# Ten pairs of k-tiles with seven products instead of eight, weight sums made by accumulating DMAs, residual kept in DRAM

## The chip, the cores and the metric

The kernel runs on one core of a Trainium2 chip. The metric is the device time of one launch in microseconds (us). The engines of the core have names in the profile: PE is TensorE (matmuls), PEld its weight loads, DVE is VectorE, ACT is ScalarE, POOL is GpSimd and SP is SyncE, which here only issues DMAs. Each engine works through its own queue in order and waits on semaphores.

## The reference

One layer of a hybrid decoder, for 256 tokens of width 2048, all in float32. A first half mixes tokens by three branches (a gated convolution, a gated MLP over chunks, a sparse attention), projects with `w_o`, normalises and adds the result to the input. The second half is the feed-forward network, and the change lies there:

```python
h = rms_norm(x, norm_ffn_pre[l])
u = causal_depthwise_conv(h @ w_up[l], ffn_conv_w[l], ffn_conv_b[l])
u_g, u_v = jnp.split(u, 2, axis=-1)
x = x + rms_norm((jax.nn.silu(u_g) * u_v) @ w_down[l], norm_ffn_post[l])
```

The product with `w_down` has 256 tokens, an inner dimension of 5632 (44 k-tiles of 128) and 2048 columns. `x` on the right of the last line is the residual: it is known before the feed-forward network begins and is needed again only at its very end.

## The kernel before, in words

Every float32 operand of a matmul is split into a rounded high part (ACT copies it into a type that TensorE runs fast) and a low part (DVE subtracts the high part from the original). A product is three matmuls: high by high, high by low, low by high. Weights arrive as tiles `wraw` of 128 x 1024 (512 KB, five buffers, fetched by SP), and the split parts go into rings `whi` and `wlo` of four buffers each. A fetch waits for the DVE step that last read the buffer five tiles before; a split waits for TensorE to finish with the ring buffer four before.

The up stage computes `h @ w_up` for 88 tiles of 128 features, two per k-tile: the convolution, `silu` and the product follow on ACT and DVE, and the result for each k-tile is stored split, in `gh` and `gl`. `fsum`, `small`, `sums` and the loop over `NFT` (L1177 to L1202) do this.

The down stage multiplies with `w_down`. Tokens are taken in two halves of 128 (`H1`, `H2`), columns in two halves of 1024 (`Pair(0)`, then `Pair(1)`), each as two blocks of 512 (`L`, `U`). A *plain* k-tile is four products (two token halves by two column blocks), 12 matmuls of 512 columns. A *quad* takes two k-tiles together: a 2 x 2 by 2 x 2 block product, which would be eight products, done with seven (the Strassen-Winograd scheme), 21 matmuls. It needs four weight arrays of 128 x 1024 at most: `b` as it lies in memory, `a` and `tt` with sums and differences, and a last half array; and, per pair, three sums and one difference of activations. Eight pairs of the 44 k-tiles are quads (`EARLY`, five pairs, and `LATE`, three), 28 tiles are plain (`PLAIN`).

The activation sums of the `EARLY` pairs are made in the up stage by `sums` and kept in `se`. There was no room for more, so those of the `LATE` pairs are made by `late` in the first column half of the down stage from `gh` and `gl`, into `sl`. The four weight combinations of a quad are made on DVE in `quad` (L1283, L1284, L1287, L1290): `b` is fetched as a `wraw` tile, `a` into `qa` (one buffer), and the combinations go into `qa` and into `tt`, one of two areas of `fin` that `scratch` gives in turn.

The order of DVE and ACT in the down stage is written out by hand (`fixed` chains each instruction behind the one before it on the engine), as is that of TensorE (`in_line`). The lists in the two loops say how many plain tiles come before each quad. The order of SP's and POOL's queues is found by the framework's scheduler. Six plain tiles of the second column half (`KEEP`) are split early and multiplied last. `combine` adds the seven products' sums up, `result` and `weigh` finish each block, and at the end the residual `y1`, which has been in SBUF since before the up stage, is added (L1402) and the output stored.

Of the kernel before, what the change touches and what calls it, by code (L numbers as in the profile page):

```python
# [20 lines left out]
F32 = mybir.dt.float32  # L24
# [10 lines left out]
NFT = FF // 128  # L35
EPS = 1e-6

EARLY = [(0, 1), (2, 3), (4, 5), (6, 7), (8, 9)]
LATE = [(11, 12), (13, 14), (15, 16)]
PLAIN = [*range(22, 33), 10, *range(17, 22), *range(33, NFT)]  # L40
BA, BB, BC, BG = 2100, 2200, 2200, 2500
PR = 1000
NW0, _ = 9, 6
# [12 lines left out]
def block(ctx: ExitStack, tc: tile.TileContext, x, xf, fp, cst, rows, sgw, w1, w2, wf_a, wt_bv, wf_bu, wf_c,  # L56
# [1054 lines left out]

    P2 = ctx.enter_context(tc.tile_pool(name="p2", bufs=1))
    P2b_ctx = ExitStack()
    se = P2.tile([128, 2, len(EARLY), 3, 128], R, name="se")
# [18 lines left out]
    with ExitStack() as order:  # L1133
        order.enter_context(tc.high_priority())
        for ins in seq[V] + seq[S]:
            order.enter_context(tc.issue_after(ins))
        junk3 = small("junk3", (128, 512), mybir.dt.bfloat16)
        for t in range(2):
            for c in range(4):
                xc = y1[:, t, c * 512:c * 512 + 512]  # L1140
                if c % 2:
                    V.scalar_tensor_tensor(junk3, xc, 1.0, xc, op0=ALU.mult, op1=ALU.mult,
                                           accum_out=ss2[:, t, c:c + 1])
                else:
                    S.activation(junk, xc, AF.Square, accum_out=ss2[:, t, c:c + 1])
        r2 = norm1(ss2, "f", 2)
    pu2.append(PS.tile([128, 2, T], F32, tag="acc", name="pu2"))
    for run in lumps(pu2[2], hs, h2):
        in_line(run)
# [15 lines left out]
    def sums(st, a0, a1, k0, dst, do=loose):  # L1165

        h, l = g2(k0, H2)
        do(V, V.tensor_add, st[:, 1], a0[:, H2], a1[:, H2])
        do(V, V.tensor_sub, st[:, 2], st[:, 1], a0[:, H1])
        do(V, V.tensor_sub, st[:, 3], a1[:, H1], st[:, 2])  # L1170
        do(S, S.activation, dst[0], st[:, 1:4], AF.Copy)
        do(V, V.tensor_sub, st[:, 0], a0[:, H1], a0[:, H2])
        do(S, S.activation, h, st[:, 0], AF.Copy)
        do(V, V.tensor_sub, dst[1], st[:, 1:4], dst[0].bitcast(F32))
        do(V, V.tensor_sub, l, st[:, 0], h.bitcast(F32))

    for i in range(NFT):  # L1177
        acc = []
        for v in range(2):
            f = 2 * i + v  # L1180
            with tc.issue_after(pe_last[0]):
                pu = pu2[f] if f < 3 else ftile(wf_up[f], h2)
            s = P2b.tile([128, T], F32, tag="fs", bufs=2, name=f"fs{f}")
            fsum(pu, s, rb=rb2)
            a = small(f"fa{f}")
            w = [fps[:, C_FW + f * 3 + k:C_FW + f * 3 + k + 1] for k in range(3)]
            S.activation(a, s, AF.Identity, bias=fps[:, C_FB + f:C_FB + f + 1], scale=w[2])
            V.scalar_tensor_tensor(a[:, 1:T], s[:, 0:T - 1], w[1], a[:, 1:T], op0=ALU.mult, op1=ALU.add)
# [4 lines left out]
        ts = H1 if i in [k for k, _ in EARLY] else slice(0, T)  # L1193
# [3 lines left out]
        for j, (k0, k1) in enumerate(EARLY):  # L1197
            if i == k0:
                first = acc[0]
            elif i == k1:  # L1200
                st = P2b.tile([128, 4, 128], F32, tag="st", name=f"st{j}")
                sums(st, first, acc[0], k0, (se[:, 0, j], se[:, 1, j]))  # L1202
    P2b_ctx.close()


# [6 lines left out]
    sl = P2c.tile([128, 2, len(LATE), 3, 128], R, name="sl")  # L1212
# [6 lines left out]
    PAIRS = EARLY + LATE  # L1219
# [23 lines left out]
    class Pair:  # L1243
# [24 lines left out]
                    in_line(self.mm, self.c[t][n], g2(PLAIN[i], (H1, H2)[t]), (hi[:, c], lo[:, c]),  # L1268
                            self.p == 0 and i == len(PLAIN) - 1)

        def quad(self, j):

            k0, k1 = PAIRS[j]
            last = j == len(PAIRS) - 1
            L, U = slice(0, 512), slice(512, 1024)
            b = fetch(wt_dq[self.p, j][:, 0:1024], 1024)
            a = P2c.tile([128, 1024], F32, name=f"qa{self.p}_{j}", tag="qa", bufs=1)
            nc.sync.dma_start(a, wt_dq[self.p, j][:, 1024:])
            nm = f"q{self.p}_{j}"
            tt = scratch()  # L1280
            (hb, lb), (ha, la), (ht, lt), (h4, l4) = (ring(nm + x) for x in "bat4")
            high(hb, b)
            fixed(V, V.tensor_sub, tt[:, L], b[:, L], a[:, U])  # L1283
            fixed(V, V.tensor_sub, a[:, U], a[:, U], a[:, L])  # L1284
            high(ha, a)
            rest(lb, b, hb)
            fixed(V, V.tensor_sub, tt[:, U], b[:, L], a[:, U])  # L1287
            high(ht, tt[:, 0:1024])
            rest(la, a, ha)
            fixed(V, V.tensor_sub, tt[:, 1024:], b[:, U], tt[:, U])  # L1290
            high(h4[:, L], tt[:, 1024:])
            rest(lt, tt[:, 0:1024], ht)
            rest(l4[:, L], tt[:, 1024:], h4[:, L])
            src, n = (se, j) if j < len(EARLY) else (sl, j - len(EARLY))
            s1, s2, s4 = ((src[:, 0, n, i], src[:, 1, n, i]) for i in range(3))
# [12 lines left out]
        def combine(self):  # L1308

            fixed(S, S.activation, self.at(0, 0), self.p1, AF.Copy)  # L1310
            fixed(V, V.tensor_add, self.at(1, 0), self.p6, self.at(0, 0))
            fixed(V, V.tensor_add, self.at(0, 1), self.p5, self.at(1, 0))
            fixed(V, V.tensor_add, self.at(1, 1), self.p7, self.at(0, 1))
            fixed(V, V.tensor_add, self.at(1, 0), self.p7, self.at(1, 0))

        def result(self, t, n, do):

# [17 lines left out]
    def late(j):  # L1335
        k0, k1 = LATE[j]
        tmp = scratch()
        a = tmp[:, 0:512].rearrange("p (k t) -> p k t", k=2)
        gi, gk = divmod(k0, 11)
        fixed(V, V.tensor_add, a, gh[gi][:, gk:gk + 2].bitcast(F32), gl[gi][:, gk:gk + 2].bitcast(F32))  # L1340
        sums(tmp[:, 512:1024].rearrange("p (s t) -> p s t", s=4), a[:, 0], a[:, 1], k0, (sl[:, 0, j], sl[:, 1, j]), fixed)

    NP, NQ, KEEP = len(PLAIN), len(PAIRS), 6


    first, second = Pair(0), None
    i = 0
    for j in range(NQ):
        while i < (6, 9, 13, 17, 19, 21, 23, 25)[j]:
            first.plain(i)  # L1350
            i += 1
        if 1 <= j <= len(LATE):
            late(j - 1)
        first.quad(j)
    for i in range(i, NP):
        first.plain(i)
# [2 lines left out]
    kept = []  # L1359
    i = 0  # L1360
    for j in range(NQ):
        while i < 3 + -((3 + KEEP - NP) * j // (NQ - 1)):
            second.plain(i)
            if i == 2:
                for t in range(2):
# [17 lines left out]
    for t in range(2):  # L1383
# [15 lines left out]
        for c in range(4):  # L1399
            for x, w in ((c * 512, 512),) if c < 3 or t == 0 else ((1536, 256), (1792, 256)):  # L1400
                cc = slice(x, x + w)
                V.scalar_tensor_tensor(res[:, t, cc], res[:, t, cc], r3, y1[:, t, cc], op0=ALU.mult, op1=ALU.add)  # L1402
                nc.sync.dma_start(out[t, :, cc], res[:, t, cc])


def _layout(inp):
# [66 lines left out]
    k0, k1 = [k for k, _ in EARLY + LATE], [k for _, k in EARLY + LATE]  # L1473
    quads = np.concatenate([dn[:, k1, 1], dn[:, k1, 0], dn[:, k0, 0], dn[:, k0, 1]], axis=3)


# [40 lines left out]
```

## Time and profile before

| | us |
|---|---|
| median of 3 runs | 1578.95 |
| lowest, highest | 1578.72, 1579.39 |
| the profiled execution, its time | 1579.09 |
| its span in the profile | 1577.3 |
| TensorE busy | 1566.0 |
| DVE busy | 1213.9 |
| ACT busy | 884.9 |
| up stage ends, down stage begins (TensorE) | 1338.2 |
| second column half begins | 1453.6 |
| last matmul of the down stage ends | 1567.9 |

The page and the views of the trace give times from the span's start. The granted TensorE clock is at full speed over the whole span. Busy times of different engines overlap. A matmul is recorded with 0.39 us, but the next one starts 0.23 us later, so the step from start to start tells more than the busy time does. In rows of tiles the three numbers behind a count are the shortest, the median and the longest of one, in ns.

### The profile page before, as it was taken

How to read it: one execution, taken by the hardware profiler on the slowest of the kernel's cores; microseconds unless marked ns; L12 is line 12 of the kernel's file. 1: busy time of each engine (PE TensorE's matmuls, PEld its weight loads, DVE VectorE, ACT ScalarE, POOL GpSimd, SP SyncE). 2: the span in 40 equal slices, each digit the busy share in tenths (PEclk: the TensorE clock that was granted, in tenths of full speed). 3: DMA queues.
4: the chain of work that ended last, by engine and by line, in shares of the span. 5: the costliest groups of instructions: out<-in, count | busy, mean ns of one | idle time of the engine just before them, and what ended most of it. 6: DMA issues, size and time to landing. Idle time of an engine off the chain costs nothing.

```text
span 1577.3 us, 22324 instructions
## 1 busy us (share of the span) xinstructions
PE 1566.0 (99%) x8185; PEld 1330.1 (84%) x8185; DVE 1213.9 (77%) x2081; ACT 884.9 (56%) x1430; POOL 18.2 (1%) x46
## 2 busy tenths in 40 slices
PE   9999999999999999999999999999999999999997
PEld 7888889888888787788888888888888888788886
DVE  8899999857865555465558988777777777888887
ACT  7544454447637675544456665555555555556563
POOL 1000020000000000000000000000000000000000
PEclk9999999999999999999999999999999999999999
DMA  9555566666765545565773666666666666656672
GB/s 376 186 192 181 186 177 213 194 192 184 235 202 152 156 145 162 161 195 183 247 242 105 203 187 189 189 191 189 192 187 191 189 191 192 204 194 214 214 243 77
DMA packets 84862, 303.74 MB, mean 193 GB/s; under 512 B 9744, under 2 KB 10768, under 8 KB 84240
## 3 DMA queue, kind: packets, MB, share of 16 engines
q1 hardware_dynamic: 83376, 297.71, 60.0%
q0 software_dynamic: 944, 4.19, 0.8%
q8 instruction: 64, 1.05, 0.3%
q10 hardware_dynamic: 432, 0.41, 0.1%
q14 instruction: 46, 0.38, 0.1%
HBM read 299.13 MB, written 2.10 MB: 191 GB/s over the span
## 4 chain that ended last, share of the span: by engine, by line
PE 98%; DVE 1%; DMA 1%; ACT 0%; issue 0%; DVEq 0%; SPq 0%; ACTq 0%
PE ps L173 29%; PE ps L180 15%; PE pd1a L1259 6%; PE pg L194 6%; PE pg L193 6%; PE pg L195 6%; PE pd0b L1259 5%; PE py L194 3%; PE py L195 3%; PE py L193 3%; PE po L195 2%; PE po L194 2%; PE po L193 2%; PE pd1b L1259 1%; PE pd0a L1259 1%; PE pv L193 1%
## 5 line engine op out<-in xcount | busy, mean ns | idle before, releaser
L145 DVE TENSOR_TENSOR wlo<-wraw,whi 128x1024 fp32r<-128x1024 f32 x440 | 534.9, 1218 | 171.6 <-ACT whi L144 164.4
L144 ACT ACTIVATE whi<-wraw 128x1024 fp32r<-128x1024 f32 x440 | 461.2, 1053 | 242.1 <-PE pg L195 96.7
L173 PE MATMUL ps<-h2T,whi 128*128 128x512 f32 x1360 | 325.0, 391 | 0.0
L173 PEld LDWEIGHTS ps<-h2T,whi 128*128 128x128 f32 x1360 | 249.8, 188 | 48.2
L180 PEld LDWEIGHTS ps<-h2T,wlo 128*128 128x128 f32 x1360 | 174.5, 191 | 6.7
L180 PE MATMUL ps<-h2T,wlo 128*128 128x256 f32 x1360 | 176.6, 283 | 0.0
L173 PE MATMUL ps<-hT,whi 128*128 128x512 f32 x640 | 157.4, 392 | 0.0
L215 ACT ACTIVATE t<-ps 128x256 f32<-128x256 f32 x125 | 47.6, 382 | 188.1 <-PE ps L173 188.0
L195 PE MATMUL pg<-whi,hT 128*128 128x512 f32 x384 | 150.9, 393 | 0.0
L194 PE MATMUL pg<-wlo,hT 128*128 128x512 f32 x384 | 150.7, 392 | 0.0
L193 PE MATMUL pg<-whi,hT 128*128 128x512 f32 x384 | 147.6, 393 | 0.0
L173 PEld LDWEIGHTS ps<-hT,whi 128*128 128x128 f32 x640 | 116.0, 189 | 21.3
L216 DVE TENSOR_TENSOR t<-ps,t 128x256 f32<-128x256 f32 x125 | 52.5, 421 | 79.0 <-ACT t L215 78.7
L476 DVE SCALAR_TENSOR_TENSOR cv<-hb,fps,cv 128x256 f32<-128x256 f32 x240 | 104.7, 475 | 0.2 <-ACT cv L472 0.2
L180 PEld LDWEIGHTS ps<-hT,wlo 128*128 128x128 f32 x640 | 84.7, 190 | 4.7
L180 PE MATMUL ps<-hT,wlo 128*128 128x256 f32 x640 | 86.8, 283 | 0.0
L194 PEld LDWEIGHTS pg<-wlo,hT 128*128 128x128 f32 x384 | 72.1, 188 | 16.1 <-issue 1.1
L195 PEld LDWEIGHTS pg<-whi,hT 128*128 128x128 f32 x384 | 72.1, 188 | 15.1 <-issue 0.7
L193 PEld LDWEIGHTS pg<-whi,hT 128*128 128x128 f32 x384 | 71.8, 188 | 14.8 <-issue 0.3
L981 DVE TENSOR_TENSOR wlowraw<-wraw,whiwraw 128x1024 fp32r<-128x1024 f32 x52 | 62.6, 1222 | 15.4 <-ACT whiwraw L981 13.8
L981 ACT ACTIVATE whiwraw<-wraw 128x1024 fp32r<-128x1024 f32 x52 | 54.7, 1059 | 22.4 <-PE pd0b L1259 7.2
L1191 ACT ACTIVATE fa<-fa 128x256 f32<-128x256 f32 x44 | 18.3, 415 | 62.5 <-DVE fa L1189 62.5
(891 smaller groups left out, 2455.4 us busy)
## 6 DMA issues: line engine op xcount, KB each, us to landing
wraw<-in_wf_up_dram SPq DMA_DIRECT2D x176, 512.0 KB, 4.3
wraw<-in_wt_g_dram SPq DMA_DIRECT2D x96, 512.0 KB, 4.3
wraw<-in_wt_dn_dram SPq DMA_DIRECT2D x56, 512.0 KB, 4.5
wraw<-in_wt_p_dram SPq DMA_DIRECT2D x48, 512.0 KB, 4.4
wraw<-in_wf_a_dram SPq DMA_DIRECT2D x32, 512.0 KB, 4.3
wraw<-in_wt_o_dram SPq DMA_DIRECT2D x32, 512.0 KB, 4.6
wraw<-in_wf_bu_dram SPq DMA_DIRECT2D x16, 512.0 KB, 4.4
wraw<-in_wf_c_dram SPq DMA_DIRECT2D x16, 512.0 KB, 4.5
```

What stands on the lines that cost most here:

```text
L144: S.activation(hi[:, :n], raw[:, :n], AF.Copy)
L145: V.tensor_sub(lo[:, :n], raw[:, :n], hi[:, :n].bitcast(F32))
L173: ins = PE.matmul(ps[:, :, ts], lhsT=ws[k // 8][0][:, c:c + 128], rhs=mov[:, k, :, ts], start=(k == 0 and not t), stop=(k == n - 1), skip_ ...
L180: ins = PE.matmul(ps[:, 1, ts], lhsT=ws[k // 8][1][:, c:c + 128], rhs=mov[:, k, 0, ts], start=False, stop=False, skip_group_check=True).ins
L193: PE.matmul(ps, lhsT=xh, rhs=hi, start=first, stop=False)
L194: PE.matmul(ps, lhsT=xh, rhs=lo, start=False, stop=False)
L195: return PE.matmul(ps, lhsT=xl, rhs=hi, start=False, stop=last).ins
L215: S.activation(t1, ps[:, 1], AF.Copy)
L216: V.tensor_add(t1 if rb is not None else dst, ps[:, 0], t1)
L476: V.scalar_tensor_tensor(ca[:, j], hb[:, j, k:k + T], w(j, k), ca[:, j], op0=ALU.mult, op1=ALU.add)
L981: seq[eng] = [op(*args, **kw).ins]
L1259: ins = PE.matmul(bank, lhsT=a[x], rhs=w[y], start=first and j == 0, stop=last and j == 2).ins
```

## The change

The pairs become ten, all with their activation sums made in the up stage; 24 k-tiles stay plain. `late` and `sl` go.

- *Room.* `y1` is written to a DRAM tensor `spill` by two DMAs of 1 MB on SP near the start of the up stage. Its place in SBUF takes `sf`, the activation sums of pairs five to nine. After the sixth quad of the second column half, in which these pairs come first, the place is free again, and the residual is read into it (`back`, two DMAs of 1 MB on SP). The second column half takes the pairs in another order for that reason.
- *Weight sums.* `qa` has three buffers. Two of the four combinations are made by DMAs that add: after `a` has been fetched, a DMA from POOL's queue adds 128 x 512 of the weights in DRAM onto its upper half; and the lower half of `tt` is fetched by SP and then added to in the same way. Each is 256 KB. To make all four combinations sums, signs move: the activation sums, two DVE steps of the quad and the last steps of `combine` change between addition and subtraction.
- *Order.* Eight plain tiles come before the first quad instead of six, and the lists that place the quads are new.

```diff
-EARLY = [(0, 1), (2, 3), (4, 5), (6, 7), (8, 9)]
-LATE = [(11, 12), (13, 14), (15, 16)]
-PLAIN = [*range(22, 33), 10, *range(17, 22), *range(33, NFT)]
+PAIRS = [(0, 1), (2, 3), (4, 5), (6, 7), (8, 9), (11, 12), (13, 14), (15, 16), (17, 18), (19, 20)]
+PLAIN = [*range(22, 33), 21, 10, *range(33, NFT)]
...
+    DR = ctx.enter_context(tc.tile_pool(name="dram", bufs=1, space=bass.MemoryType.DRAM))
+    spill = DR.tile([128, 2, D], F32, name="spill")
+    for t in range(2):
+        nc.sync.dma_start(spill[:, t], y1[:, t])
+    sf = P0.tile([128, 2, 5, 3, 128], R, tag="s16", name="sf")
...
-        do(V, V.tensor_add, st[:, 1], a0[:, H2], a1[:, H2])
+        do(V, V.tensor_sub, st[:, 1], a0[:, H2], a1[:, H2])
...
-        do(V, V.tensor_sub, st[:, 3], a1[:, H1], st[:, 2])
+        do(V, V.tensor_add, st[:, 3], a1[:, H1], st[:, 2])
...
-        def quad(self, j):
+        def quad(self, n):
+            j = (n + 5 * self.p) % len(PAIRS)
...
-            a = P2c.tile([128, 1024], F32, name=f"qa{self.p}_{j}", tag="qa", bufs=1)
+            a = P2c.tile([128, 1024], F32, name=f"qa{self.p}_{j}", tag="qa", bufs=3)
             nc.sync.dma_start(a, wt_dq[self.p, j][:, 1024:])
+            G.dma_start(a[:, U], wt_dq[self.p, j][:, 1024:1536], accum_op=ALU.add)
             nm = f"q{self.p}_{j}"
             tt = scratch()
+            nc.sync.dma_start(tt[:, L], wt_dq[self.p, j][:, 1536:])
+            G.dma_start(tt[:, L], wt_dq[self.p, j][:, 0:512], accum_op=ALU.add)
...
-            fixed(V, V.tensor_sub, tt[:, L], b[:, L], a[:, U])
-            fixed(V, V.tensor_sub, a[:, U], a[:, U], a[:, L])
...
-            fixed(V, V.tensor_sub, tt[:, U], b[:, L], a[:, U])
+            fixed(V, V.tensor_add, tt[:, U], b[:, L], a[:, U])
...
-            fixed(V, V.tensor_sub, tt[:, 1024:], b[:, U], tt[:, U])
+            fixed(V, V.tensor_add, tt[:, 1024:], b[:, U], tt[:, U])
...
-        while i < (6, 9, 13, 17, 19, 21, 23, 25)[j]:
+        while i < (8, 9, 11, 13, 14, 16, 17, 19, 20, 21)[j]:
...
-        if 1 <= j <= len(LATE):
-            late(j - 1)
...
-        while i < 3 + -((3 + KEEP - NP) * j // (NQ - 1)):
+        while i < (3, 5, 7, 9, 10, 12, 14, 15, 17, 18)[j]:
...
+        if j == 5:
+            back = s16(P0, [128, 2, D], F32, "back")
+            for t in range(2):
+                nc.sync.dma_start(back[:, t], spill[:, t])
...
-                V.scalar_tensor_tensor(res[:, t, cc], res[:, t, cc], r3, y1[:, t, cc], op0=ALU.mult, op1=ALU.add)
+                V.scalar_tensor_tensor(res[:, t, cc], res[:, t, cc], r3, back[:, t, cc], op0=ALU.mult, op1=ALU.add)
```

More of the change, by code (lines that the diff above doesn't have):

```diff
@@ L1113, in block @@
     P2b_ctx = ExitStack()
-    se = P2.tile([128, 2, len(EARLY), 3, 128], R, name="se")
+    se = P2.tile([128, 2, 5, 3, 128], R, name="se")
     gh = [P2.tile([128, 11, T], R, tag="gh", bufs=4, name=f"gh{i}") for i in range(4)]
@@ L1192, in block @@
         V.tensor_mul(acc[0], acc[0], acc[1])
-        ts = H1 if i in [k for k, _ in EARLY] else slice(0, T)
+        ts = H1 if i in [k for k, _ in PAIRS] else slice(0, T)
         h, l = g2(i, ts)
@@ L1196, in block @@
         V.tensor_sub(l, acc[0][:, ts], h.bitcast(F32))
-        for j, (k0, k1) in enumerate(EARLY):
+        for j, (k0, k1) in enumerate(PAIRS):
             if i == k0:
@@ L1201, in block @@
                 st = P2b.tile([128, 4, 128], F32, tag="st", name=f"st{j}")
-                sums(st, first, acc[0], k0, (se[:, 0, j], se[:, 1, j]))
+                sums(st, first, acc[0], k0, [(se, sf)[j // 5][:, x, j % 5] for x in range(2)])
     P2b_ctx.close()
@@ L1211, in block @@
     gain = fin[:, 4096:5120]
-    sl = P2c.tile([128, 2, len(LATE), 3, 128], R, name="sl")
     turn = [0]
@@ L1217, in scratch @@
         return fin[:, 5120 + 1536 * turn[0]:6656 + 1536 * turn[0]]
-    PAIRS = EARLY + LATE
     ss3 = PZ.tile([128, 2, 8], F32, name="ss3")
@@ L1269, in plain @@
                             self.p == 0 and i == len(PLAIN) - 1)
-        def quad(self, j):
+        def quad(self, n):
+            j = (n + 5 * self.p) % len(PAIRS)
             k0, k1 = PAIRS[j]
-            last = j == len(PAIRS) - 1
+            last = n == len(PAIRS) - 1
             L, U = slice(0, 512), slice(512, 1024)
             b = fetch(wt_dq[self.p, j][:, 0:1024], 1024)
-            a = P2c.tile([128, 1024], F32, name=f"qa{self.p}_{j}", tag="qa", bufs=1)
+            a = P2c.tile([128, 1024], F32, name=f"qa{self.p}_{j}", tag="qa", bufs=3)
             nc.sync.dma_start(a, wt_dq[self.p, j][:, 1024:])
+            G.dma_start(a[:, U], wt_dq[self.p, j][:, 1024:1536], accum_op=ALU.add)
             nm = f"q{self.p}_{j}"
             tt = scratch()
+            nc.sync.dma_start(tt[:, L], wt_dq[self.p, j][:, 1536:])
+            G.dma_start(tt[:, L], wt_dq[self.p, j][:, 0:512], accum_op=ALU.add)
             (hb, lb), (ha, la), (ht, lt), (h4, l4) = (ring(nm + x) for x in "bat4")
             high(hb, b)
-            fixed(V, V.tensor_sub, tt[:, L], b[:, L], a[:, U])
-            fixed(V, V.tensor_sub, a[:, U], a[:, U], a[:, L])
             high(ha, a)
             rest(lb, b, hb)
-            fixed(V, V.tensor_sub, tt[:, U], b[:, L], a[:, U])
+            fixed(V, V.tensor_add, tt[:, U], b[:, L], a[:, U])
             high(ht, tt[:, 0:1024])
             rest(la, a, ha)
-            fixed(V, V.tensor_sub, tt[:, 1024:], b[:, U], tt[:, U])
+            fixed(V, V.tensor_add, tt[:, 1024:], b[:, U], tt[:, U])
             high(h4[:, L], tt[:, 1024:])
@@ L1293, in quad @@
             rest(l4[:, L], tt[:, 1024:], h4[:, L])
-            src, n = (se, j) if j < len(EARLY) else (sl, j - len(EARLY))
-            s1, s2, s4 = ((src[:, 0, n, i], src[:, 1, n, i]) for i in range(3))
+            src = (se, sf)[j // 5]
+            s1, s2, s4 = ((src[:, 0, j % 5, i], src[:, 1, j % 5, i]) for i in range(3))
             for bank_, act, (h, l), c in (
@@ L1311, in combine @@
             fixed(V, V.tensor_add, self.at(1, 0), self.p6, self.at(0, 0))
-            fixed(V, V.tensor_add, self.at(0, 1), self.p5, self.at(1, 0))
-            fixed(V, V.tensor_add, self.at(1, 1), self.p7, self.at(0, 1))
+            fixed(V, V.tensor_sub, self.at(0, 1), self.p5, self.at(1, 0))
             fixed(V, V.tensor_add, self.at(1, 0), self.p7, self.at(1, 0))
+            fixed(V, V.tensor_sub, self.at(1, 1), self.at(0, 1), self.p7)
         def result(self, t, n, do):
@@ L1333, in weigh @@
             do(V, V.tensor_mul, self.at(t, n), self.at(t, n), gain[:, n * 512:n * 512 + 512])
[L1335 to L1341, printed above, removed]
     NP, NQ, KEEP = len(PLAIN), len(PAIRS), 6
@@ L1472, in _layout @@
     plain = c(dn[:, PLAIN].transpose(0, 1, 3, 2, 4)).reshape(2, len(PLAIN), 128, 1024)
-    k0, k1 = [k for k, _ in EARLY + LATE], [k for _, k in EARLY + LATE]
+    k0, k1 = [k for k, _ in PAIRS], [k for _, k in PAIRS]
     quads = np.concatenate([dn[:, k1, 1], dn[:, k1, 0], dn[:, k0, 0], dn[:, k0, 1]], axis=3)
```

## The prediction

> **What bounds the kernel now.** I read the page's busy times first, then the chain of work that ended last, then busy times by stretches, and last the tiles of the stage that the change rewrites.
>
> ```profile
> span 1577.3 us, 22324 instructions
> PE 1566.0 (99%) x8185; PEld 1330.1 (84%) x8185; DVE 1213.9 (77%) x2081; ACT 884.9 (56%) x1430; POOL 18.2 (1%) x46
> PE 98%; DVE 1%; DMA 1%; ACT 0%; issue 0%; DVEq 0%; SPq 0%; ACTq 0%
> ```
>
> TensorE works for 1566.0 of 1577.3 us and makes up 98% of the chain. So a matmul removed is time won, and a transfer, a DVE or an ACT step costs nothing until TensorE waits for it. The chain in the last stage (columns: start, length, what):
>
> ```profile
> 1338.23 5.46 PE pd0b L1259 x24
> ...
> 1346.47 5.64 DMA qa<-in_wt_dq_dram
> ...
> 1352.23 0.70 DVE fin L981
> ...
> 1358.31 1.43 PE pd0a L1259 x5
> ...
> 1453.61 9.52 PE pd1a L1259 x42
> 1463.13 2.72 PE pd1b L1259 x12
> ...
> 1550.85 17.01 PE pd1a L1259 x75
> ...
> 1567.88 0.42 DVE fin L1326
> ```
>
> The stage runs from 1338.23 to 1567.86; column half 1 begins at 1453.61. Twelve matmuls take 2.72 us, so one takes 0.2267. A plain k-tile is 12 matmuls (2.72 us), a quad, which covers two k-tiles with seven products, is 21 (4.76 us).
>
> ```profile
> core 0: us, PE busy (x) PEld busy (x) DVE busy (x) ACT busy (x) POOL busy (x), PEclk, DMA share, GB/s
> 14.00:40.00 26.00, 26.00 (x116) 21.56 (x115) 24.59 (x50) 21.88 (x50) 5.78 (x9) 1.00 1.01 409
> 1338.23:1453.61 115.38, 115.17 (x505) 94.30 (x505) 98.43 (x124) 63.31 (x71) 0.00 (x0) 1.00 0.64 204
> 1453.61:1567.86 114.25, 114.24 (x504) 94.25 (x503) 97.00 (x117) 62.85 (x76) 0.00 (x0) 1.00 0.57 185
> ```
>
> Each half holds 28 plain tiles and 8 quads: 336 + 168 = 504 matmuls, 504 x 0.2267 = 114.25 us. The second half takes exactly that; the first takes 115.38, so 1.13 us are lost in it. Their place shows in TensorE's own rows around the first quad:
>
> ```profile
> 1354.16 0.39 PE L1259 MATMUL pd0b<-whiwraw,gl 128*128 128x512 f32 x1
> 1354.39 0.39 PE L1259 MATMUL pd0b<-whiq_0b,se 128*128 128x512 f32 x1
> 1354.84 0.50 PE L1259 MATMUL pd0b<-wloq_0b,se 128*128 128x512 f32 x1
> ```
>
> The step from 1354.39 to 1354.84 is 0.45, not 0.23: TensorE waits for the first quad's pieces, which are late because the array `qa` landed at 1352.11 (1346.47 + 5.64) and DVE stood until then. The busy sum hardly shows it, as a matmul's 0.39 overlaps the next.
>
> **The change part by part.** *Matmuls.* Ten pairs and 24 plain tiles make 288 + 210 = 498 matmuls a half, 112.89 us, against 504. Twelve matmuls go, on the path: -2.72 us.
>
> *The start of the stage.* Eight plain tiles precede the first quad in place of six. The products of `a` are then due at 1338.23 + 8 x 2.72 + 1.36 = 1361.35. What delivers `a` gets a further hop: SP issues the three `qa` fetches at the same place as before, behind one weight fetch, and POOL then issues a DMA that adds 256 KB onto its upper half. No accumulating transfer is in the trace. Its bounds are POOL's own transfers and the fetches:
>
> ```profile
> L981 DVE TENSOR_TENSOR qa<-qa x16: 691/692/694, 1353.0 to 1542.6; 128x512 f32<-128x512 f32 x16
> L981 DVE TENSOR_TENSOR fin<-wraw,qa x32: 680/684/691, 1352.2 to 1544.3; 128x512 f32<-128x512 f32 x32
> DMA to landing us min/median/max: 3.6/3.8/5.6
> ...
> L937 POOL DMA_DIRECT2D x<-in_x_dram x2: 537/542/548, 755.2 to 755.7; - x2
> DMA to landing us min/median/max: 7.1/8.7/10.2
> ...
> DMA to landing us min/median/max: 2.0/4.0/5.5
> ...
> DMA to landing us min/median/max: 3.5/4.5/5.7
> ```
>
> (Landings in this order: `qa`, 512 KB; `x2`, 1 MB from POOL; `kd`, 64 KB from POOL; `wraw`, 512 KB, in this stage.)
>
> ```profile
> L981 DVE TENSOR_TENSOR wlowraw<-wraw,whiwraw 128x1024 fp32r<-128x1024 f32 x49 | 59.0, 1222 | 13.8 <-ACT whiwraw L981 12.1
> L981 ACT ACTIVATE whiwraw<-wraw 128x1024 fp32r<-128x1024 f32 x49 | 51.5, 1059 | 19.2 <-PE pd0b L1259 7.2 <-PE pd1a L1259 2.9 <-PE pd1b L1259 2.4
> ```
>
> With POOL's 0.54 to issue and 4.0 to land (64 KB) `a` is whole at 1356.6, and after ACT's 1.06 and DVE's 1.22 its pieces at 1358.9: 2.4 us early. With 8.7 (1 MB) they come at 1363.6, 2 us late. 256 KB is nearer the first, so I take no wait, and the 1.13 us come back: -1.13. Ends: -1.13 to +0.9.
>
> *DVE and ACT.* Two of four subtractions go from each quad: 0.69 + 0.68 = 1.37 us less DVE work, against five more pairs' sums in the up stage (below) and none late. DVE keeps idling in this stage, and ACT's steps per quad stay as they were. Both cost nothing.
>
> *The queues.* SP issues 24 DMAs more over the kernel (20 for `tt`, four for the residual; four more `qa` and four fewer weight fetches cancel), POOL 40. Each quad gains one SP issue (256 KB into `tt`) and two POOL issues (0.54 each, 21.7 us for 40 on an engine that is idle here). On SP the `tt` fetch of a quad waits for the last DVE step of the quad two before, and what stands behind it are fetches whose buffers DVE frees later still, so the wait delays nothing by itself. `tt` is then two quads and about three plain tiles (over 15 us of TensorE) ahead of its use, against 3.8 + 0.54 + 4.0 = 8.3 us for both hops: 7 us of cover.
>
> *The bytes.* This is the price that decides. At the start of the kernel the 16 DMA engines are full and move 409 GB/s: 1.28 us for 512 KB, 0.64 for 256 KB. Let an accumulating transfer cost f times a plain one. The lower end is f = 1, its bytes alone; it reads two operands and writes one, so three passes in a row, f = 3, is the upper end. The two reads share the read side and the write can overlap, as it does in a copy, so f = 2 is my value. From the first quad to the last, half 0 needs 13 plain tiles and ten quads: (13 x 0.524 + 10 x 1.311 MB) / 409 = 48.7 us and 20 accumulations, 12.8 f, against 13 x 2.72 + 10 x 4.76 = 83.0 us of TensorE. At f = 2 that is 74.3: it fits. Half 1 needs 19 tiles, ten quads, a gain row and the residual's return (2.10 MB): 62.8 + 12.8 f against 15 x 2.72 + 47.6 = 88.4 us. At f = 2 that is 88.4: just full.
>
> The Trainium skill, "DMA: Bandwidth & Descriptors", section "Two DMAs through the same engine are not ordered", reports that a read-modify-write packet often read data older than the packet ahead of it would leave, so such packets overlap. That speaks for two passes and against a full round trip per packet; no run here shows it. The same page's Specifications give an HBM limit of about 358 GB/s per core: by it half 1 would need 101 us, and the sum would be about 1581. The 409 GB/s measured here disagrees, so that rule gets no chance of its own.
>
> *The reload.* `back`, 2 MB in one piece on SP after the sixth quad of half 1, takes 5.1 us of the queue. A weight tile is fetched when the tile five before is split and split itself when TensorE frees a ring slot: 5 x 2.72 - 1.06 - 1.22 = 11.3 us later, less 4.5 to land: 6.8 us of cover. The reload leaves 1.7. If one quad's two accumulations at f = 2 and its extra 256 KB (2.56 + 0.64 = 3.2) pass in between, the next tile is 1.5 us late. Ends: 0 (nothing between) and 6 (half 1 at f = 3: 101.2 - 88.4 - 6.8). I take +1.5.
>
> *The up stage.*
>
> ```profile
> L971 DVE SCALAR_TENSOR_TENSOR y<-y,rsyo,x x4: 745/746/753, 830.7 to 832.7; 128x512 f32<-128x512 f32 x4
> L981 DVE SCALAR_TENSOR_TENSOR y<-y,rsyo,x x4: 740/746/752, 847.8 to 852.7; 128x512 f32<-128x512 f32 x4
> ...
> 838.67 0.33 SPq L104 DMA_DIRECT2D wraw<-in_wf_up_dram  x1
> 854.61 0.33 SPq L104 DMA_DIRECT2D wraw<-in_wf_up_dram  x1
> ...
> 862.39 1.09 ACT L144 ACTIVATE whi<-wraw 128x1024 fp32r<-128x1024 f32 x1
> wraw<-in_wf_up_dram SPq DMA_DIRECT2D x176, 512.0 KB, 4.3
> ...
> 900.00:960.00 60.00, 60.00 (x349) 53.07 (x348) 52.46 (x97) 35.82 (x63) 0.00 (x0) 1.00 0.64 191
> ```
>
> The two spills of `y1` (1 MB each) wait on SP for rows complete at 833.4 and 853.4, ahead of fetches that go out at 838.67 and 854.61 anyway. The second puts 2.6 us of queue before a tile that ACT takes at 862.39: 854.61 + 4.3 + 2.6 = 861.5, hidden by 0.9. Five more sums ride on DVE in stretches like 900 to 960, where five pairs already do so with TensorE at 60.00 of 60. Zero; without that cover the spill would cost up to 1.7.
>
> **Sum.** 1579.09 (the profiled execution) - 2.72 - 1.13 + 1.5 = 1576.74. That execution stands 0.14 above the median of 1578.95, so the forecast is 1576.6, 0.15% below. A measurement tells about 0.2%, 3.2 us, from no change: the bounds are 1575.8 and 1582.1.
>
> **The rivals.** *All hidden.* The accumulations cost little over their bytes (f below 1.8) and nothing passes beside the reload: 1578.95 - 3.85 = 1575.1, faster by 0.24%. For it: the stage now uses 0.64 and 0.57 of the DMA engines. Against: half 1 is full at f = 2. Chance 0.27.
>
> *My forecast*, 1576.6, own range 1575.8 to 1581.1 (f = 3). Chance 0.34.
>
> *The first quad stays late*: the accumulation takes 8.7 us; the 1.13 stay and 0.9 is added, 1578.6, no change. Against: only a transfer four times larger took so long. Chance 0.06.
>
> *Slower: the DMA engines become the bound.* At f = 3.5 half 0 needs 93.5 us against 83.0, half 1 107.6 against 88.4; less 6.8 of cover each, 3.7 + 12.4 = 16.1 us of waiting: 1578.95 - 3.85 + 16.1 = 1591.2. At f = 4 it is 1604. It beats the gain from f = 2.8 and passes 0.2% from f = 3.1, or earlier if the queue, fed in bursts here, stays below 409 GB/s. Nothing in the trace excludes it, since it holds no such transfer. Chance 0.33.
>
> **How the numbers follow.** Faster 0.27; same 0.34 + 0.06 = 0.40; slower 0.33. The range runs from a little below the all-hidden case, 1574.9, to 1591.2; what it leaves out is f above 3.5, under 2 in 10.
>
> **What would show it.** Right: 8173 matmuls; no double step in TensorE's rows at the first quad; half 0 at 112.9 us, half 1 a microsecond or two more, with the gap right after `back`; a DMA share in the stage of 0.85 or more; accumulations landing in 4 to 6 us. Wrong: DVE or ACT waiting for a DMA into `fin` or `qa` at quad after quad and both halves well above 112.9 (the slower rival), or landings near 9 us at the first quad alone.

## The result, and the profile after

The changed kernel takes 1586.09 us (median of 6 runs, 1583.84 to 1587.04) against 1578.99 for the kernel before (6 runs on the same chip): 1.0042 times as long, 95% interval 1.0032 to 1.0052. Forecast was 1576.6. The profiled execution has 1586.25 us, 7.16 above that of the kernel before.

The page of the changed kernel: its span, its busy times, the engines' shares of the chain.

```profile
span 1584.5 us, 22491 instructions
PE 1568.1 (99%) x8173; PEld 1329.8 (84%) x8173; DVE 1208.1 (76%) x2074; ACT 891.1 (56%) x1442; POOL 53.3 (3%) x86
PE 95%; DMA 3%; DVE 1%; ACT 1%; issue 0%; SPq 0%; DVEq 0%; ACTq 0%; POOLq 0%
```

The twelve matmuls are gone (8173 for 8185), yet the chain now holds 3% of DMA instead of 1%. The two column halves of the down stage by stretches (columns as in the prediction's table of stretches: after the length come PE, PEld, DVE, ACT and POOL busy, then the granted clock, the DMA share and GB/s):

```profile
1338.36:1459.39 121.03, 116.84 (x500) 95.32 (x499) 87.96 (x95) 63.75 (x69) 21.96 (x25) 0.97 0.96 278
1459.39:1575.53 116.14, 114.46 (x499) 92.76 (x497) 92.64 (x109) 65.53 (x80) 13.16 (x15) 1.00 0.78 249
```

498 matmuls need 112.89 us. Half 0 loses 8.14 us and half 1 3.25. The stage begins 0.13 later than before, and what follows the last matmul is 0.47 shorter, 8.97 for 9.44. The DMA share of half 0 went from 0.64 to 0.96, and its clock is 0.97: a stretch of it did not run at full speed. The chain of waits shows where time went (start, length, what; the line numbers of the products and fetches are four or five higher than before):

```profile
1338.36 5.45 PE pd0b L1263 x24
1346.64 8.89 DMA qa<-in_wt_dq_dram
1356.28 7.09 DMA qa<-in_wt_dq_dram
1365.90 5.06 PE pd0a L1263 x11
...
1438.77 7.87 DMA fin<-in_wt_dq_dram
...
1511.28 13.69 DMA wraw<-in_wt_dq_dram
```

Three places: the first quad, whose `a` makes two hops (the fetch, then POOL's addition); the last quad of half 0, whose `tt` is late; and the `b` tile behind the residual's reload in half 1. TensorE's rows at the first quad:

```profile
1361.09 0.39 PE L1263 MATMUL pd0b<-whiq_0b,gl 128*128 128x512 f32 x1
1364.64 0.50 PE L1263 MATMUL pd0a<-whiq_0a,gh 128*128 128x512 f32 x1 [3.16 <-ACT whiq_0a L981]
1365.90 0.80 PE L1263 MATMUL pd0a<-wloq_0a,gh 128*128 128x512 f32 x1 [0.76 <-DVE wloq_0a L981]
1366.49 0.63 PE L1263 MATMUL pd0a<-whiq_0a,gl 128*128 128x512 f32 x1
1366.92 0.63 PE L1263 MATMUL pd0a<-whiq_0a,se 128*128 128x512 f32 x1
...
1371.61 0.56 PE L1263 MATMUL pd0b<-whiq,gl 128*128 128x512 f32 x1
1372.01 0.40 PE L1263 MATMUL pd0b<-whiwraw,gh 128*128 128x512 f32 x1
```

The step 1361.09 to 1364.64 is 3.55 instead of 0.23: 3.32 lost. The next, 1.26, loses 1.03. Then 14 steps from 1365.90 to 1372.01 take 6.11 us instead of 3.17, 2.94 lost, and no wait is recorded in them: the first takes 0.59, the last 0.40, all others 0.43 (0.63 recorded). TensorE itself is slow there, as the granted clock in these stretches says:

```profile
1366.00:1371.50 5.50, 5.50 (x13) 4.35 (x14) 5.22 (x6) 3.13 (x4) 0.34 (x1) 0.50 0.81 242
1372.00:1376.00 4.00, 4.00 (x19) 3.29 (x18) 3.29 (x4) 1.75 (x3) 0.89 (x2) 1.00 0.76 153
```

The same 14 steps take 3.68 to 3.70 us in the four runs below whose clock stayed at 1.00 behind a wait at this place (e4, e8, e10, e13), so about 2.4 of the 2.94 us are the clock's; the other 0.5 are lost at full clock too.

So 3.32 + 1.03 + 2.94 = 7.3 of the 8.14 us sit at the first quad; of the rest 0.6 are at the last quad and 0.2 at the seventh, both at products of `tt`.

### The profile page after: what moved, and what is told of

The parts are those of the page before. It is cut to its first block, busy times and chain, and to the rows that moved or that the text cites. A ratio compares the mean times of both kernels' runs of the same rounds, so it can differ in the third digit from the quotient of the medians.

```text
span 1584.5 us, 22491 instructions
## 1 busy us (share of the span) xinstructions
PE 1568.1 (99%) x8173; PEld 1329.8 (84%) x8173; DVE 1208.1 (76%) x2074; ACT 891.1 (56%) x1442; POOL 53.3 (3%) x86
## 4 chain that ended last, share of the span: by engine, by line
PE 95%; DMA 3%; DVE 1%; ACT 1%; issue 0%; SPq 0%; DVEq 0%; ACTq 0%; POOLq 0%
PE ps L173 29%; PE ps L180 15%; PE pg L194 6%; PE pg L193 6%; PE pg L195 6%; PE pd1a L1263 4%; PE pd0b L1263 4%; PE py L194 3%; PE py L195 3%; PE py L193 3%; PE po L193 2%; PE po L194 2%; PE po L195 2%; PE pd0a L1263 2%; PE pd1b L1263 1%; DMA qa<-in_wt_dq_dram 1%
## 5 line engine op out<-in xcount | busy, mean ns | idle before, releaser
L981 DVE TENSOR_TENSOR wlowraw<-wraw,whiwraw 128x1024 fp32r<-128x1024 f32 x44 | 53.1, 1223 | 17.4 <-ACT whiwraw L981 16.6
L981 ACT ACTIVATE whiwraw<-wraw 128x1024 fp32r<-128x1024 f32 x44 | 46.2, 1058 | 23.5 <-PE pd0b L1263 10.7
L1193 ACT ACTIVATE fa<-fs,fps 128x256 f32<-128x256 f32 x88 | 52.5, 596 | 1.1 <-DVE fs L218 0.9
```

Of the source, the lines that this page charges most:

```text
L981: seq[eng] = [op(*args, **kw).ins]
```

## The experiments

All are edits of the changed kernel, timed beside the kernel before, whose median was 1579.1 to 1579.5 there. Where the text speaks of theories A, B and C, they are those of the expectation of that run; A in the first four (e1, e3, e3b, e4) is the wait at the first quad with the clock that follows from it. Half lengths are from the profiled executions, the ideal being 112.9 each.

| run | median us | ratio to before, 95% | half 0 | half 1 | DMA share, half 0 |
|---|---|---|---|---|---|
| changed kernel | 1586.09 | 1.0042 (1.0032 to 1.0052) | 121.03 | 116.14 | 0.96 |
| e1 first quad's sums on DVE | 1579.42 | 0.9999 (0.9991 to 1.0008) | 113.87 | 116.65 | 0.98 |
| e3 nine tiles ahead | 1582.70 | 1.0021 (1.0012 to 1.0029) | 118.46 | 115.79 | 0.96 |
| e3b eleven tiles ahead | 1583.47 | 1.0029 (1.0018 to 1.0039) | 118.34 | 116.11 | 0.98 |
| e8 `a` fetches in turn | 1585.23 | 1.0037 (1.0025 to 1.0050) | 118.17 | 115.30 | 0.98 |
| e4 14 unused matmuls | 1584.32 | 1.0040 (1.0026 to 1.0054) | 118.66 | 116.44 | 0.98 |
| e13 5 unused matmuls | 1583.84 | 1.0032 (1.0020 to 1.0044) | 117.63 | 116.31 | 0.98 |
| e7 copies, not additions | 1579.99 | 1.0002 (0.9993 to 1.0011) | 115.29 | 113.90 | 0.90 |
| e2 all sums on DVE | 1576.85 | 0.9986 (0.9977 to 0.9994) | 112.90 | 114.05 | 0.67 |
| e11 `a` on DVE, `tt` added by DMA | 1577.13 | 0.9988 (0.9979 to 0.9997) | 113.25 | 114.68 | 0.89 |
| e10 reload last | 1582.23 | 1.0018 (1.0009 to 1.0027) | 117.74 | 112.93 | 0.98 |
| e5 = e1, reload in four | 1576.97 | 0.9984 (0.9976 to 0.9993) | 114.19 | 113.90 | 0.99 |
| e6 = e1, reload last | 1576.76 | 0.9980 (0.9971 to 0.9989) | 114.03 | 113.81 | 0.98 |
| e9 = e2, reload last | 1576.77 | 0.9985 (0.9976 to 0.9993) | 112.88 | 114.06 | 0.68 |
| e12 = e11, reload last | 1574.80 | 0.9973 (0.9963 to 0.9983) | 112.91 | 113.01 | 0.90 |

### The first quad

e1, the first quad alone without its additions:

```diff
+            adds = not (self.p == 0 and n == 0)
+            if adds:
+                G.dma_start(a[:, U], wt_dq[self.p, j][:, 1024:1536], accum_op=ALU.add)
...
+            if adds:
+                nc.sync.dma_start(tt[:, L], wt_dq[self.p, j][:, 1536:])
+                G.dma_start(tt[:, L], wt_dq[self.p, j][:, 0:512], accum_op=ALU.add)
...
             high(hb, b)
+            if not adds:
+                fixed(V, V.tensor_add, tt[:, L], b[:, L], a[:, U])
+                fixed(V, V.tensor_add, a[:, U], a[:, U], a[:, L])
             high(ha, a)
```

> The two added sums of the first quad of column half 0 are made on DVE again, from `a` and `b`; the other 19 quads keep their accumulating DMAs. Theory A (the loss sits at the first quad: POOL's hop makes `a` 3.3 us late, the next pieces 1.0 us, and TensorE then runs at half clock for 2.9 us): `a` lands at about 1355.5 as in the changed kernel, DVE needs 1.4 us, ACT 1.06 and DVE 1.22 behind it, so the products of `a` find their pieces at 1359.3, before 1361.35. Half 0 falls from 121.0 to 114 us, the clock stays at 1.00, the time is 1579 to 1580. Theory B (the 16 DMA engines are the bound and the first quad only shows it first): the waits move to the second and third quad, half 0 stays above 118 us, the time is 1583 to 1586. Theory C (the clock drops at that place for another reason than the wait): 2.9 us stay, about 1582.5.

1579.42 us; half 0 loses 1.0 instead of 8.1, and the clock is 1.00 all through the stage. One quad of twenty carried nearly all of half 0's loss, though the DMA share there was as high as before, 0.98. B and C fail here.

e3 changes only the first entries of the list, and e3b (11, 12, 13, 14, 15, 16, 17, 19, 20, 21) some more:

```diff
-        while i < (8, 9, 11, 13, 14, 16, 17, 19, 20, 21)[j]:
+        while i < (9, 10, 11, 13, 14, 16, 17, 19, 20, 21)[j]:
```

> Nine plain tiles before the first quad instead of eight, the second quad after the tenth as its list entry; nothing else. Theory A: the products of `a` are due 2.72 us later, so the waits shrink from 3.3 + 1.0 to about 1 to 1.5 us, too short for the clock to fall: half 0 about 115.5, time about 1580.5. Theory B: what the first quad no longer waits for the next ones do, since the bytes are the same: half 0 above 118, time 1584 or more. Theory C: the clock falls all the same: about 1583.

> Eleven plain tiles before the first quad, the following quads one tile apart; nothing else. Theory A: 8.2 us more for the first quad, no wait there and no fall of the clock: half 0 loses at most 2 us (the quads behind stand closer), time 1578 to 1580. Theory B: the quads stand closer together, so the DMA engines are asked for more per microsecond: half 0 above 119, time 1585 or more.

Both miss theory A's numbers (1580.5; 1578 to 1580); their times lie between the theories, and half 0 of e3, 118.46, is where B put it. The first quad's waits are as A says: 0.39 and 0.75 in e3, none in e3b, clock 1.00. But both still lose about 5.5 us in half 0. By TensorE's steps 2.1 of e3's 5.6 us are still at the first quad and 3.4 at products of `tt` of later quads; in e3b all 5.4 are at `tt` of the fourth, sixth and last quad. From the chain of e3b:

```profile
1338.28 31.28 PE pd0b L1263 x138
1376.83 6.91 DMA fin<-in_wt_dq_dram
1384.35 9.24 DMA fin<-in_wt_dq_dram
1401.07 8.45 DMA fin<-in_wt_dq_dram
...
```

So B is half right. With all accumulations in place the DMA engines have nothing to spare: most of what a later first quad saves, the closer quads behind it lose. That the gap at the late first quad also gave the later ones time is not shown: e1 has no gap there, and its later quads, at the old distances, lose only 1.0.

Why was the first hop 8.89 us, where the kernel before has 5.64? e8 tests whether the three `a` fetches issued together are the reason:

```diff
+            if self.p == 0 and n in (1, 2):
+                with tc.issue_after(added[0]):
+                    G.memset(a[:, 0:1], 0.0)
             nc.sync.dma_start(a, wt_dq[self.p, j][:, 1024:])
...
+            if not added:
+                added.append(ins)
```

Here `ins` is the addition that POOL issues onto `a`.

> As the changed kernel, but the `a` fetches of the second and third quad wait until POOL has issued the addition onto the first quad's `a` (POOL writes one column of their buffers behind it, and the fetch must follow that); all accumulating DMAs stay. Theory A, first hop (`a` of the first quad lands 8.9 us after its issue, not 5.6, because three `a` fetches go out together): it lands at 1352.5 to 1353.5 as in the kernel before, the addition lands at 1360 to 1361, TensorE waits under 1 us instead of 4.3 and its clock stays at 1.00; the second quad's `a`, fetched from 1354, is whole at about 1368 and costs up to 1 us. Half 0 from 121.0 to 114.5 to 116, time 1579.5 to 1581.5. Rival (the addition's 0.9 us on POOL and 7 us to land are enough by themselves, or the two additions onto `tt` slow the first fetch): `a` lands at 1355 again, half 0 stays above 119, time above 1584.

The rival holds: with the other two `a` fetches held back until 1357, the first still took 7.97 us, and the 0.9 us of the median are within the spread of the runs. (Half 0 is 118.17 and not above 119, as in the profiled execution the first wait was 1.3 us shorter and the clock held, of which more below.) In e2 three such fetches go out together but nothing moves for `tt`, and the first is read by DVE at 1351.8, 5.7 after its issue. In e7, where `tt` gets copies in place of additions, it took 8.64. So it is the traffic for `tt` ahead of it, added or copied, that delays the first hop. The 4 us in which the first fetch goes out, in e2 and then in the changed kernel:

```profile
1346.00:1350.00 4.00, 4.00 (x19) 3.30 (x19) 1.33 (x2) 2.12 (x2) 0.00 (x0) 1.00 0.71 181
```

```profile
1346.00:1350.00 4.00, 4.00 (x20) 3.30 (x19) 1.72 (x3) 1.73 (x2) 1.83 (x2) 1.00 0.91 292
```

The next 4 us, in the kernel before and in the changed one:

```profile
1350.00:1354.00 4.00, 4.00 (x20) 3.30 (x19) 1.73 (x3) 0.18 (x1) 0.00 (x0) 1.00 0.21 81
```

```profile
1350.00:1354.00 4.00, 4.00 (x19) 3.34 (x18) 2.08 (x2) 1.45 (x2) 0.00 (x0) 1.00 0.95 274
```

Before, the queue had emptied (share 0.21); now it is full (0.95). This second pair alone would prove little, since the two further `a` fetches fill these 4 us in e2 too (share 1.01), where the first fetch has landed in time.

### The clock

e4 keeps TensorE from idling while it waits, with products that nobody uses; e13 has five in place of fourteen:

```diff
+                if self.p == 0 and n == 0 and bank_ is self.p1:
+                    for _ in range(14):
+                        in_line(lambda: PE.matmul(self.p6, lhsT=act[0], rhs=hb[:, U], start=True, stop=True).ins)
```

> Fourteen matmuls that nobody uses (3.2 us at 0.2267) stand in TensorE's queue ahead of the first quad's products of `a`, in the bank that p6 overwrites later; no wait and no transfer is changed. Theory A (the half clock follows from the 3.3 us wait): TensorE is busy while it would have waited, the clock stays at 1.00, the 14 steps of 0.43 become 0.23, and the kernel with more work is 2.5 to 3 us faster than the changed kernel: about 1583.3. Theory C (the clock falls for another reason, or the arrays come at that pace): the half clock stays, 1586 to 1589.

> The changed kernel with five unused matmuls (1.1 us) instead of fourteen ahead of the first quad's products of `a`. They shorten TensorE's idle stretch from 3.2 to about 2.1 us and move nothing else: the wait ends at the same time. If the clock falls with the length of the idle stretch (it fell after 3.16 us and did not after 2.38 in another run), it stays at 1.00 and the time is that of fourteen, 1583 to 1584.3. If any wait at this place lowers it, or the sum of both waits, half clock from 1365 to 1371 and about 1586.

With more work the medians are lower, 1584.32 (a microsecond above what A expected) and 1583.84 against 1586.09. But the ratios to the kernel before, 1.0040 and 1.0032 against 1.0042, have intervals that overlap, so the gain in time is not clear of the noise. Both profiles keep the clock at 1.00 behind the wait, but `a` also came sooner in them than in the profile of the changed kernel: without the extra matmuls the waits would have been about 2.7 us in e4 and 2.3 in e13, so the profiles alone don't show that the matmuls kept the clock. The mean clocks of the runs speak for it in e4: 0.998 in four of its six, 0.997 and 0.999 in the others, against 0.996 to 0.998 of the changed kernel. The row of e4 for the stretch that ran at 0.50, and the first late product in e13 and in e10 (nothing changed there before half 1):

```profile
1366.00:1371.50 5.50, 5.42 (x24) 4.15 (x23) 5.50 (x7) 4.00 (x5) 0.53 (x1) 1.00 0.84 256
```

```profile
1363.47 0.50 PE L1263 MATMUL pd0a<-whiq_0a,gh 128*128 128x512 f32 x1 [1.18 <-ACT whiq_0a L981]
```

```profile
1363.80 0.50 PE L1263 MATMUL pd0a<-whiq_0a,gh 128*128 128x512 f32 x1 [2.38 <-ACT whiq_0a L981]
```

After a wait of 3.16 us the clock halved; after 2.38 (e10), 1.89 (e8), 1.18 (e13) it did not, though a second wait of 0.76 followed in each. The fall and the return in the changed kernel:

```profile
1365.10:1365.15 0.05, 0.04 (x1) 0.00 (x0) 0.05 (x1) 0.05 (x1) 0.00 (x0) 0.77 0.22 41
1371.95:1372.00 0.05, 0.05 (x1) 0.00 (x0) 0.00 (x0) 0.05 (x1) 0.05 (x1) 0.96 1.10 451
```

The clock fell at 1365.1, half a microsecond after the first late product had started, and came back at about 1371.95: 6.8 us at half rate. In these four executions the longest wait is the one that cost the clock. One fall does not fix the edge, nor does it tell whether the first wait alone counts or both together. A small difference in landing can decide: in six profiled executions with the `tt` traffic ahead of it (the changed kernel, e3, e4, e8, e10, e13) the first hop took 7.9 to 9.0 us. That fits the spread of runs of one kernel. The six of the changed kernel spread over 3.2 us, the lowest at a mean clock of 0.998 and the highest at 0.996; the profiled executions of e8 and e10 are the fastest of theirs, 2.0 and 2.5 us below the median. The Trainium skill, "TensorE: Matmul & The Clock Gate", section "Part 1: The HAM clock gate", says that an idle window of about 3.4 us halves the clock, that a busy one of about 3.4 us brings it back, and that the window runs free of the program. The trace agrees in part: the 6.8 us at half rate are two such windows, but the 3.4 us ahead of the fall were not all idle, as they hold the half microsecond of the first product. If the window runs free, where a wait falls in it may decide as much as its length; no run here separates the two. The page's step at half rate, 426.7 ns for 512 columns, agrees with 0.43.

### What adding costs

e7 drops the adding and keeps its forty DMAs:

```diff
-            G.dma_start(a[:, U], wt_dq[self.p, j][:, 1024:1536], accum_op=ALU.add)
+            G.dma_start(a[:, U], wt_dq[self.p, j][:, 1024:1536])
...
-            G.dma_start(tt[:, L], wt_dq[self.p, j][:, 0:512], accum_op=ALU.add)
+            G.dma_start(tt[:, L], wt_dq[self.p, j][:, 0:512])
```

> POOL's forty DMAs copy instead of adding (so the weight sums, and the output, are other numbers): same issues, same bytes written, same order. It prices the adding by itself. If an accumulation costs two plain transfers, the DMA share of half 0 falls from 0.96 to about 0.83, landings of POOL's DMAs from 6.6 and 8.0 us to 4 to 5, `a` is whole 2.5 us earlier, the first quad waits under 1.5 us without a fall of the clock: half 0 about 115.5 us, half 1 about 115, time about 1579.5. If adding costs nothing over copying (the hop and POOL's queue are what costs): half 0 stays above 119, time 1584 or more.

1579.99: the 6.1 us are due to adding rather than copying, the fall of the clock included, which e7 does not have. Queues of the down stage, changed kernel first, then e7 (packets, MB, share of 16 engines over 237.17 and 229.19 us; q0 is POOL's):

```profile
q1 hardware_dynamic: 15698, 51.91, 61.3%
q0 software_dynamic: 5760, 10.49, 25.6%
```

```profile
q1 hardware_dynamic: 15701, 51.91, 65.2%
q0 software_dynamic: 3200, 10.49, 14.6%
```

10.49 MB take 0.256 x 237.17 = 60.7 us of the engines when added and 0.146 x 229.19 = 33.5 when copied: 1.81 times; per MB, against SP's plain transfers of the same execution, 2.07 times. POOL needs 0.87 us to issue one against 0.55. Medians from issue to landing fall from 6.6 and 8.0 us to 5.2 and 6.5, less than expected, and the share to 0.90, not 0.83.

e2 undoes the additions alone (`adds` false everywhere), e11 those onto `a`:

> All four sums of every quad on DVE, no accumulating DMA and no fetch into `tt`; ten pairs, the spill, the reload, the three `qa` buffers and the lists stay. Theory A2 (what the accumulating DMAs cost is more than the DVE work they save): half 0 falls from 121.0 to between 113 and 114.5 us, the DMA share of the stage falls below 0.65, the reload finds free engines and half 1 needs 113 to 114.5; the time is 1576 to 1578.5, faster than the kernel before. Rival D (DVE needs the relief): 24 x 1.22 + 10 x 7.0 = 99 us of DVE work in 113 us, with quads one tile apart, make DVE the engine that TensorE waits for at the closer quads: half 0 above 115.5 and half 1 above 115, the time 1580 or more.

> The sum in `a` on DVE in all quads; `tt` is still fetched and added to by DMAs; reload as in the changed kernel. Theory A (the added hop on `a` is what costs, as `a` has the least time; `tt` has 15 us): half 0 falls to 113 to 114 us with a DMA share near 0.85, half 1 stays at 115 to 116 with the reload, time 1577.5 to 1579. Theory B (either accumulation is too much for the queue): half 0 above 116, time 1581 or more.

In e2 half 0 reaches the ideal, 112.90, with eight tiles ahead and no wait. Theory A2 holds for it but for the DMA share, 0.67 and not below 0.65; half 1 loses 1.15. e11 is as A expected, a little better: with one addition per quad, the one that has time, half 0 loses 0.36.

### The reload

```diff
             back = s16(P0, [128, 2, D], F32, "back")
-            for t in range(2):
-                nc.sync.dma_start(back[:, t], spill[:, t])
...
     assert i == NP - KEEP and len(kept) == KEEP
+    for t in range(2):
+        with tc.issue_after(fetched[0]):
+            nc.sync.dma_start(back[:, t], spill[:, t])
```

This is e10, and e6, e9, e12 on the bases of the table; e5 has four pieces of 512 KB, each behind the `b` fetch of one of the last four quads.

> The changed kernel with the reload behind the last weight fetch and nothing else changed. Theory A (the parts add up): half 0 stays at 121, half 1 falls from 116.1 to 113.5 to 114, time 1583.5 to 1584.2. Theory B (full DMA engines: what the reload no longer takes, the accumulations do): half 1 stays above 115, 1585 to 1586.

> As the run with the first quad's sums on DVE (1579.4), and the residual comes back in four pieces of 512 KB, one behind the `b` fetch of each of the last four quads, instead of two of 1 MB together. Theory A (the 3.7 us that half 1 loses are the 2 MB ahead of the next quad's `b` fetch): a piece of 512 KB fits the 6.8 us of cover, half 1 falls from 116.6 to 113.5 to 114.5, the time to 1577 to 1578. Theory B (half 1 loses them because its DMA engines are full, whatever the place): the waits spread over the last quads, half 1 stays at 116 or more, 1579 to 1581.

> As the run with the first quad's sums on DVE (1579.4), and the residual's two 1 MB fetches stand behind the last weight fetch. Theory A and theory B agree on half 1: no weight waits for them, so it falls from 116.6 to 113 to 114 us. They land at about 1550 to 1555, 12 us before the last matmul ends, so the tail stays at 9 us: time 1576 to 1577. If half 1 still needs 115.5 or more, its loss isn't the reload but the accumulating transfers themselves.

> All four sums of every quad on DVE, no accumulating DMA, and the reload behind the last weight fetch; ten pairs and the lists as in the changed kernel. Theory A (what half 1 lost with all sums on DVE, 1.2 us, is the reload): half 0 stays at 112.9, half 1 comes to 112.9 to 113.3 and the time to 1575.2 to 1576.2, faster than both kernels. Rival D (it is DVE, busy 39.5 of 40 us around the reload): half 1 stays at 114, 1576.8.

In e10 half 1 falls by 3.2 us to the ideal, better than expected, and the tail does not grow. Its half 0 misses the 121, as the first wait was 0.8 us shorter in that execution and the clock held. e5 and e6 do alike on the base of e1: 2.8 us won in half 1. e9 misses theory A: moving the reload does nothing where all sums are on DVE (114.05, 114.06). There the loss is DVE. About 0.8 of its 1.15 us follow one wait, and DVE works without a gap for ten us before it:

```profile
1530.13 2.35 DVE L981 TENSOR_TENSOR wlowraw<-wraw,whiwraw 128x1024 fp32r<-128x1024 f32 x2
```

```profile
1531.40 0.50 PE L1263 MATMUL pd1a<-wlowraw,gh 128*128 128x512 f32 x1 [0.51 <-DVE wlowraw L981]
```

The relief of one step per quad in e12 removes that loss. So the reload costs nothing on a queue without additions (e2 to e9), 1.7 us with half of them (e11 to e12) and 3.2 with all.

> The sum in `a` on DVE in all quads, `tt` still fetched and added to by DMAs, and the reload behind the last weight fetch. Theory A (with the hop on `a` gone and the reload out of the way nothing is left in the stage but matmuls): half 0 113.3 as in the run with `a` on DVE, half 1 falls from 114.7 to 113 to 113.5, time 1575.5 to 1576.3, below both kernels. Rival (the limit in half 1 is the closely set last quads, on DVE or on the DMA engines): half 1 stays at 114 or more, 1576.8 to 1577.5.

e12 is faster than both kernels and than A expected, 1574.80 us, 0.27% below the kernel before; its halves are 112.91 and 113.01:

```profile
1337.86:1450.77 112.91, 112.91 (x500) 93.46 (x499) 93.31 (x105) 65.05 (x69) 10.57 (x12) 1.00 0.90 270
1450.77:1563.78 113.01, 113.00 (x499) 93.08 (x497) 98.14 (x119) 66.63 (x80) 7.02 (x8) 1.00 0.75 238
```

Ten pairs are worth what the count of matmuls says once two things are mended. Of the accumulating DMAs those onto `tt` earn about 2 us (e9 to e12), those onto `a` cost about 7 (e12 to e10, 7.4), with the waits and, in runs that meet it, the clock at the first quad.

## Why the prediction was wrong

Its sum for the profiled execution was 1576.74; measured 1586.25, 9.51 more. By its own terms: half 0, taken as free of loss, +8.14; reload, 3.25 for 1.5, +1.75; stage start +0.13; tail -0.47; what lies around the span -0.04. These make 9.51.

- *Matmuls, -2.72.* Right: 8173, and e12 shows the halves at 112.9 and 113.0.
- *The start of the stage, -1.13.* The step that failed. "SP issues the three `qa` fetches at the same place as before" was right (1346.64 for 1346.47), that the fetch lands as before was not: 8.89 us for 5.64, as `tt`'s transfers fill a queue that was empty. The second hop was taken as 0.54 + 4.0; it was 0.75 until POOL issued, then 7.09 from issue to landing, with adding under load. That is 3.25 and 3.30 us too little on two hops in a row, against a reserve of 2.4: 4.15 late, and the two waits lost 3.32 + 1.03 = 4.35. The other half of that step, that eight tiles ahead recover the 1.13, is right when nothing hops (e2).
- *The rival "first quad stays late"* named the right place, and its 8.7 us landing was not far from 7.09. Its price, +0.9 beside the 1.13, left out the delay of the first hop and that a wait of 3.16 us is paid again in clock: 2.94 us in the steps behind it, about 2.4 of them the clock's. No term of the sum stood for the clock. Its chance of 0.06 rested on size alone (64 KB or 1 MB), without the load on the queue.
- *Bytes: f = 2.* Right: 1.8 to 2.1. *409 GB/s* was not, for this stage. From 1400 to 1460 the changed kernel has a share of 0.99 to 1.00 at 291 to 293 GB/s; SP's plain transfers alone come to 51.91 MB in 61.3% of 237.17 us, 357 GB/s. The trace of before had said so: 204 GB/s at a share of 0.64 is 319 at a full one. With that, half 0 is full, not at 74.3 of 83.0 us.
- *The Trainium skill's figure of 358 GB/s* ("DMA: Bandwidth & Descriptors", Specifications), which the prediction set aside for the 409 of the kernel's start, is near the 357 of this stage; but e7 moves 413 in a slice of the same stage, so no run shows it as a limit.
- *Queues: 7 us of cover for `tt`.* Measured medians are 6.8 + 0.87 + 8.0 = 15.7 us for both hops, against 15 us: no cover. It showed as 0.8 us at two quads, and where quads stand closer as 3.4 us in e3 and 5.4 in e3b.
- *Reload, +1.5.* Mechanism right (the gap is at the next `b` tile, 13.69 us after its issue, and e10 removes it), the size half of it, inside the stated 0 to 6.
- *DVE, ACT, the up stage: 0.* Right here; DVE is the next bound, as e2 and e9 show.
- *The rival "DMA engines the bound"* (1591.2 at f = 3.5) came nearest in time and is half the cause: the engines are full, but by f = 2 at a lower rate, and the loss sits at three places, not at quad after quad.

## What to carry to other kernels

A chain of dependent transfers is to be costed at the load that the change itself puts on the queue at that moment, not at the landing times of the old trace; and a queue's capacity is the GB/s of the stage divided by its busy share, not the best slice of the kernel. A long wait of TensorE can have a second price: here one of 3.16 us cost about 2.4 us more in clock and one of 2.38 none, so by these two a microsecond less can win three. Where a step moves from an engine to a DMA, move it for the operands that have time (`tt`), not for the first one that is awaited (`a`); and a bulk reload goes behind the last fetch that anything waits for.

## What the runs showed of the hardware

- TensorE's granted clock fell to 0.50 half a microsecond after a wait of 3.16 us in the middle of a kernel and stayed there for 6.8 us; after 2.38, 1.89 and 1.18 us it stayed at 1.00. Whether unused matmuls during the wait keep the clock, and make the kernel faster, is not settled: the runs with fourteen of them (e4) have mean clocks of 0.997 to 0.999 against 0.996 to 0.998, but the times are not clear of the noise.
- An accumulating DMA of 256 KB costs the engines 1.81 times a copy from the same queue, and 0.87 us of POOL's time to issue against 0.55. Forty of them take 5760 packets where forty copies take 3200.
- Three 512 KB fetches at once did not slow the first of them (5.7 us, e2); 256 KB transfers into another buffer, issued ahead of it or together with it, did (7.9 to 9.0).
